# Output projection's first steps in old pools and its last group in another order; a beginning by half channels with eight buffers

## The chip, the cores and the metric

One of the eight cores of a Trainium2 chip runs the whole kernel. The metric is device time in microseconds. A core has five engines that run side by side and meet by semaphores: TensorE (PE) multiplies matrices into PSUM, VectorE (DVE) and ScalarE (ACT) work element by element, GpSimd (POOL) takes smaller work, and SyncE (SP) issues most DMAs. ACT and POOL can issue DMAs too. Each engine executes its own instructions strictly in order.

## The reference

One step of a layer for a prompt of 1024 rows and 8 samples of 8 rows each (1088 rows, 1024 channels, float32):

```
mod = silu(c) @ w_ada + b_ada                     # 6 sections of 1024 columns
h   = rms_norm(x) * (1 + scale1) + shift1
p   = h @ w_in                                    # z, xbc, dt | qkv, gate, beta, alpha
y   = SSD scan of silu(conv(xbc)), gated by silu(z), grouped norm     # 1024 rows of "mixed"
o   = gated delta rule of silu(conv(qkv)), norm, gated by silu(gate)  # the other 1024
x   = x + gate1 * rms_norm(concat(y, o) @ w_out)
x   = x + gate2 * rms_norm(swiglu(modulated norm of x) @ w_down)
```

It returns x and the new convolution and recurrent states of prompt and samples.

## The kernel before

Activations lie with channels on the 128 partitions, rows along the free axis, in three groups of rows TH of 384, 384 and 320 (the last ends with the 64 sample rows). A float32 product is made of three matmuls: activations and weights are each split into a rounded high part and the remaining low part (hh, hl and wh, wl), and high x high, low x high and high x low are added in PSUM. The split of weights is a cast on ACT (L173) and a subtraction on DVE (L174).

**Order.** PE's instructions run in the order in which the program text issues them (manual_schedule). For the other engines a scheduler orders them; earlier program text has higher priority, and an instruction without open dependences can be placed far ahead of its text. Side work is written as generators in `tasks`; every `tick()`, called at fixed places between matmuls, moves each of them on by one `yield`.

**Beginning.** c, the first three x tiles, w_ada's first four column blocks (2 MB each) and the first weights are loaded by SP; the w_ada tiles `w2` have 12 buffers. `ada_block` makes a block's 512 columns of mod, `ada_cols` (L304) turns them into modT. `turned` (L339) transposes x tiles, `modulated` (L357 to L368) makes hh and hl: one ACT pass, one or two DVE passes, and the low part on DVE (even k) or POOL (odd k). The first two column tiles of w_in (`first`: k and q of head 0) are multiplied while h is still being made: PE runs block 0, block 2, transpositions of channels 0 to 3, block 1, matmuls of channels 0 to 3 (`first_k`, L416 to L418), block 3, then channels 4 to 7. For groups two and three `first_group` interleaves, channel by channel, three transpositions, the modulation and six matmuls two channels behind. `few` adds the small parameters and the halo rows of the convolution (36 small transpositions, L391).

**Output projection.** `gemm_rows` goes through three groups of rows. A group has 16 steps; step k takes 128 rows of the mixed result (`mixed_load` from DRAM, L1331), splits them (sh, sl; L1398, L1399) and multiplies them with two halves of w_out's rows (`w_out_half`, casts L173): 18 matmuls a step (L1386 to L1389), fewer in the last group, and four ticks. All groups go k = 8 to 15 first (the delta rule's), then 0 to 7 (the scan's; these need a multiply by the group norm, L1458). Weights of even k use pool wp, of odd k pool wo; pieces of even k use pool mxp, of odd k g_. wo and g_ lie where the scan's tiles were. `gdn_samples`, the delta rule for the samples, runs in the ticks of groups one and two, and its result is read from DRAM by group three.

Of the kernel before, what the change touches and what calls it, by code (L numbers as in the profile page):

```python
# [8 lines left out]
F32 = mybir.dt.float32  # L9
# [7 lines left out]
P = 128  # L17
# [26 lines left out]
def hybrid_step(ctx: ExitStack, tc: tile.TileContext, x_p, x_s, c_p, c_s, st_ssd, st_ssdc, st_gdn, st_gdnc,  # L44
# [34 lines left out]
    warm = cA.tile([1, 1], F32, name="warm")  # L79
    dve.memset(warm, 0.0)  # L80
    act.activation(out=warm, in_=warm, func=AF.Silu)
# [77 lines left out]
    def bank():  # L159
        return bg[0].tile([P, 512], F32, name="ps")  # L160
# [73 lines left out]
    sp.dma_start(out=cc[0:1, :], in_=c_p)  # L234
    sp.dma_start(out=cc[1:9, :], in_=c_s)
    sp.dma_start(out=cc[9:10, :], in_=n_mix_pre)
# [13 lines left out]
    def load_x(i):  # L250
        n = P if i < NC else NS
        if i >= 4:
            xts.append(init.tile([P, 2, 512], F32, name="w2", bufs=12).rearrange("p a n -> p (a n)"))
        xt = xts[i]
        sp.dma_start(out=xt[0:n], in_=x_p[i * P:(i + 1) * P, :] if i < NC else x_s)
# [9 lines left out]
    for i in range(3):  # L265
        load_x(i)
# [12 lines left out]
    w2s = {}  # L279

    def load_ada(cb):
        w2s[cb] = []
        for k in range(0, KD, 2):
            w2 = init.tile([P, 2, 512], F32, name="w2", bufs=12)
            sp.dma_start(out=w2, in_=w_ada[k * P:(k + 2) * P, cb * 512:(cb + 1) * 512]
                         .rearrange("(a p) n -> p a n", p=P))
            w2s[cb].append(w2)
# [28 lines left out]
    def load_params():  # L316
        sp.dma_start(out=r1[0:8, :], in_=n_mix_pre[0].rearrange("(r c) -> r c", c=P))
        sp.dma_start(out=r1[8:16, :], in_=n_ffn_pre[0].rearrange("(r c) -> r c", c=P))
        sp.dma_start(out=r1[16:24, :], in_=ssd_nw[0].rearrange("(r c) -> r c", c=P))
        sp.dma_start(out=r1[24:25, :], in_=gdn_nw)  # L320
        sp.dma_start(out=r1[25:37, :], in_=ssd_cb[0].rearrange("(r c) -> r c", c=P))
        sp.dma_start(out=r1[37:85, :], in_=ssd_cw[0].rearrange("j (r c) -> (j r) c", c=P))
        sp.dma_start(out=r2, in_=gdn_cw[0].rearrange("j (r c) -> (j r) c", c=P))

    def params():
        ps = bank()
        pe.transpose(ps[:, 0:85], r1[0:85, :], ident[0:85, 0:85])
        pe.transpose(ps[:, 128:224], r2, ident[0:96, 0:96])
        dve.tensor_copy(prm1T, ps[:, 0:85])
        dve.tensor_copy(prm2T, ps[:, 128:224])  # L330
        yield
# [40 lines left out]
    def mod(g, k, ps):  # L372
        c0, n = TH[g]
        modulated(ps, k, c0, n, hh[k][:, c0:c0 + n], hl[k][:, c0:c0 + n], init, pool if k % 2 else dve)


    HALOS = ((st_ssdc[0], 0, 8), (st_ssdc[0], 8, 4), (st_gdnc[0], 0, 8), (st_gdnc[0], 8, 8), (st_gdnc[0], 16, 8))
    sts = []

    def load_halos():  # L380
        for src, a, n in HALOS:
            st = init.tile([P, 2, 512], F32, name="w2", bufs=12).rearrange("p a n -> p (a n)")[0:24, 0:n * P]
            sp.dma_start(out=st, in_=src[:, :, a * P:(a + n) * P].rearrange("b t c -> (b t) c"))
            sts.append(st)

    def halos():
        for st, (src, a, n) in zip(sts, HALOS):
# [24 lines left out]
    def first_k(g, k, pss):  # L412
        t0, n = TH[g]
        xh, xl = hh[k][:, t0:t0 + n], hl[k][:, t0:t0 + n]
        for (hi, lo), o in zip(first, pss):
            pe.matmul(o, lhsT=hi[k], rhs=xh, start=(k == 0), stop=False)  # L416
            pe.matmul(o, lhsT=hi[k], rhs=xl, start=False, stop=False)
            pe.matmul(o, lhsT=lo[k], rhs=xh, start=False, stop=(k == KD - 1))  # L418

    def first_group(g):  # L420

        pss = [ps_a.tile([P, 512], F32, name="ps")[:, 0:TH[g][1]] for _ in first]
        for k in range(KD + 2):
            if k < KD:
                mod(g, k, turned(g, k))
            if k >= 2:
                first_k(g, k - 2, pss)
                tick()
        hid_box[g] = clock[0]
        return pss  # L430

    load_ada(0)
    load_ada(2)
    for load in loads:
        load(0)
    load_ada(1)
    rows = ada_block(0)
    load_ada(3)
    for load in loads:
        load(1)  # L440
# [3 lines left out]
    tps = [turned(0, k) for k in range(4)]  # L444
    ada_cols(2, rows2)
    for k in range(4):
        mod(0, k, tps[k])
    rows = ada_block(1)
    for k in range(2):
        first_k(0, k, first_ps)  # L450
    ada_cols(1, rows)
    for k in range(2, 4):
        first_k(0, k, first_ps)
    rows2 = ada_block(3)
    for i in range(3, NT):
        load_x(i)
    load_params()
    load_halos()

    wsr = gk.tile([P, 4, NS], F32, name="sm").rearrange("p a t -> p (a t)").rearrange("p (k m) -> p k m", m=32)  # L460
    for a, b, c in ((0, 16, C_DT), (16, 24, C_ALPHA), (24, 32, C_BETA)):
        sp.dma_start(out=wsr[:, :, a:b], in_=w_in[:, c:c + b - a].rearrange("(k p) m -> p k m", p=P))
    tps = [turned(0, k) for k in range(4, KD)]
    ada_cols(3, rows2)
    for k in range(4, KD):
        mod(0, k, tps[k - 4])
    with tc.high_priority(-80):
        for i in range(3, NT):
            norm_x(i)
    for k in range(4, KD):  # L470
        first_k(0, k, first_ps)
    hid_box[0] = clock[0]
    wst = gk.tile([P, NP], F32, name="gate")[:, 0:KD * 64].rearrange("p (k m) -> p k m", m=64).bitcast(F32R)

    def rate_weights():
        pool.memset(wst.bitcast(F32), 0.0)
        act.copy(wst[:, :, 0:32], wsr)
        dve.tensor_sub(wst[:, :, 32:64], wsr, wst[:, :, 0:32].bitcast(F32))
        yield

    def few():

        yield from wait(6)
        yield from params()
        yield from halos()
        yield from rate_weights()

    few_run = few()
    spawn(few_run)

# [476 lines left out]
    def first_two(wts):  # L967

        raws = [conv_raw() for _ in wts]
        pss = first_ps  # L970
        for g in range(3):
            if g:
                pss = first_group(g)
            t0, n = TH[g]
            for ps, raw in zip(pss, raws):
                raw[2](ps, t0, n, min(n, NP - t0))
        settle(few_run)
# [351 lines left out]
    def mixed_load(k, c0, n):  # L1329
        t = (g_ if queue and k % 2 else mxp).tile([P, 384], F32, name="mx", bufs=3)  # L1330
        sp.dma_start(out=t[:, 0:n], in_=mixdr[k * P:(k + 1) * P, c0:c0 + n])  # L1331
        return t

# [13 lines left out]
    KS = list(range(KD, 2 * KD)) + list(range(KD))  # L1347

    queue, last = [(k, *TH[gi]) for gi in range(2) for k in KS], []
    for i in range(4):  # L1350
        ahead.append(mixed_load(*queue.pop(0)))
# [111 lines left out]
    def gdn_samples():  # L1463
        smx = g_.tile([P, HG, 4, NS], F32, name="smx")
        sp.dma_start(out=smx, in_=smdr)
# [10 lines left out]
        yield from wait(16)  # L1476
# [238 lines left out]

    def w_out_half(k, hf):
        return load_half(w_out[k * P:(k + 1) * P, hf * 512:hf * 512 + 512], wp=wo if k % 2 else wp)

    ph_f = ExitStack()
    for gi, grp in enumerate(GRP):  # L1720
# [22 lines left out]
        gemm_rows(grp, KS, w_out_half, mixed_piece(c0, n), mid, done)  # L1743
        if gi == 1:
            settle()
            last += [(k, *TH[2]) for k in KS]
            for i in range(2):
                ahead.append(mixed_load(*last.pop(0)))
# [224 lines left out]
```

## Time and profile before

| | |
|---|---|
| time, median of 3 runs | 2013.7 us (2012.06 to 2014.39) |
| profiled execution: time, span | 2012.82 us, 2011.0 us |
| PE busy, share of the span | 1951.5 us, 97% |
| DVE, ACT, POOL busy | 67%, 51%, 6% |
| mean granted clock of PE | 0.987 of 2.4 GHz |
| moved by DMA, over the span | 117 GB/s |

Matmuls overlap, so PE busy over a stretch says that it had work, not how fast it went; what a stream of them costs is the distance of their starts. A line of the timeline gives the start, the duration, the engine, the line of the program, the operation, the tiles written and read, and in brackets the idle time before it and what ended it. PEclk is 1.00 at 2.4 GHz and 0.50 at 1.2 GHz.

### The profile page before, as it was taken

What the parts mean: (1) busy time and instruction counts of PE and PEld (TensorE: products, weight loads), DVE (VectorE), ACT (ScalarE), POOL (GpSimd) and SP (SyncE); (2) the same over time, 40 slices, a digit from 0 to 9 for tenths busy, and PEclk for the clock granted to TensorE, in tenths of its full rate; (3) what the DMA queues carried; (4) which work ended last, traced back from release to release, by engine and by line L of the source; (5) the groups of instructions that cost most, each with busy time, mean ns of one, the idle gap of its engine ahead of it and who ended that gap; (6) DMA issues with size and microseconds to landing.
All of it is one profiled execution on the core that took longest, in us unless ns stands there. A gap on an engine that the chain in (4) does not pass through costs nothing.

```text
span 2011.0 us, 35475 instructions
## 1 busy us (share of the span) xinstructions
PE 1951.5 (97%) x13211; PEld 1753.8 (87%) x13211; DVE 1351.1 (67%) x2964; ACT 1035.2 (51%) x2578; POOL 125.9 (6%) x184
## 2 busy tenths in 40 slices
PE   6999999999999999999969999999999999999998
PEld 4898899999999998998857677899999999988886
DVE  4669767877887766867657767885555556645465
ACT  4455455554655446777435666753333334544454
POOL 2100000000000001100011010100000000000000
PEclk9799999999999999999989999999999999999999
DMA  8223323322211127555267855422222224633131
GB/s 300 56 60 102 97 81 110 100 81 87 84 52 55 59 83 189 177 138 159 77 212 228 258 184 192 127 75 81 75 76 82 76 81 128 225 125 110 46 100 50
DMA packets 223142, 235.29 MB, mean 117 GB/s; under 512 B 19018, under 2 KB 177252, under 8 KB 222842
## 3 DMA queue, kind: packets, MB, share of 16 engines
q1 hardware_dynamic: 220266, 228.86, 36.8%
q10 hardware_dynamic: 2384, 3.05, 0.4%
q8 instruction: 104, 1.70, 0.3%
q0 software_dynamic: 320, 1.12, 0.2%
q14 instruction: 68, 0.56, 0.1%
HBM read 188.83 MB, written 44.15 MB: 116 GB/s over the span
## 4 chain that ended last, share of the span: by engine, by line
PE 84%; DVE 6%; ACT 3%; DMA 3%; issue 2%; SPq 1%; POOL 1%; DVEq 0%; POOLq 0%; ACTq 0%
PE ps L198 9%; PE ps L199 8%; PE ps L200 8%; PE ps L1874 7%; PE ps L1873 7%; PE ps L1875 7%; PE ps L1386 7%; PE ps L1389 7%; PE ps L1388 6%; PE ps L741 2%; PE ps L795 1%; DMA wr<-in_w_out_dram 1%; PE ps L704 1%; DVE uc L891 1%; DMA L<-accr 1%
## 5 line engine op out<-in xcount | busy, mean ns | idle before, releaser
L198 PE MATMUL ps<-hh,wh 128*128 128x384 f32 (+1 forms) x1200 | 425.6, 355 | 0.1
L200 PE MATMUL ps<-hh,wl 128*128 128x384 f32 (+1 forms) x1200 | 393.0, 327 | 0.0
L199 PE MATMUL ps<-hl,wh 128*128 128x384 f32 (+1 forms) x1200 | 392.6, 327 | 0.0
L1386 PE MATMUL ps<-wh,sh 128*128 128x512 f32 x678 | 274.6, 405 | 16.0 <-ACT wh L173 15.2
L1389 PE MATMUL ps<-wl,sh 128*128 128x512 f32 x678 | 267.7, 395 | 0.2 <-DVE wl L174 0.2
L198 PEld LDWEIGHTS ps<-hh,wh 128*128 128x128 f32 x1200 | 227.1, 189 | 17.1 <-issue 11.5
L1388 PE MATMUL ps<-wh,sl 128*128 128x512 f32 x604 | 237.6, 393 | 3.7 <-DVE sl L1399 3.7
L199 PEld LDWEIGHTS ps<-hl,wh 128*128 128x128 f32 x1200 | 227.3, 189 | 0.8
L200 PEld LDWEIGHTS ps<-hh,wl 128*128 128x128 f32 x1200 | 226.0, 188 | 0.0
L173 ACT CAST wh<-wr 128x512 fp32r<-128x512 f32 x200 | 122.7, 621 | 171.0 <-PE ps L199 84.5
L174 DVE TENSOR_TENSOR wl<-wr,wh 128x512 fp32r<-128x512 f32 x200 | 136.8, 691 | 58.5 <-ACT wh L173 57.8
L1386 PEld LDWEIGHTS ps<-wh,sh 128*128 128x128 f32 x678 | 128.4, 189 | 52.4 <-ACT wh L173 15.6
L174 DVE TENSOR_TENSOR wl<-wd,wh 128x512 fp32r<-128x512 f32 x130 | 89.6, 692 | 118.1 <-ACT wh L173 114.8
L1389 PEld LDWEIGHTS ps<-wl,sh 128*128 128x128 f32 x678 | 128.4, 189 | 30.3 <-DVE wl L174 0.8
L173 ACT CAST wh<-wd 128x512 fp32r<-128x512 f32 x130 | 80.7, 621 | 139.0 <-PE ps L1388 100.3
L1388 PEld LDWEIGHTS ps<-wh,sl 128*128 128x128 f32 x604 | 114.5, 190 | 27.3 <-DVE sl L1399 4.5
L1810 ACT CAST wh<-s 128x512 fp32r<-128x512 f32 x104 | 64.4, 620 | 83.1 <-PE ps L1874 74.6
L1873 PE MATMUL ps<-T_0h,wh 128*128 128x272 f32 x352 | 102.0, 290 | 3.3 <-DVE u L1889 1.8
L1874 PE MATMUL ps<-T_0l,wh 128*128 128x272 f32 x352 | 101.6, 289 | 0.0
L1874 PE MATMUL ps<-T_1l,wh 128*128 128x272 f32 x352 | 101.6, 289 | 0.0
L1875 PE MATMUL ps<-T_0h,wl 128*128 128x272 f32 x352 | 101.3, 288 | 0.0
L1875 PE MATMUL ps<-T_1h,wl 128*128 128x272 f32 x352 | 101.3, 288 | 0.0
(496 smaller groups left out, 4442.6 us busy)
## 6 DMA issues: line engine op xcount, KB each, us to landing
wr<-in_w_in_dram SPq DMA_DIRECT2D x104, 256.0 KB
wr<-in_w_gate_up_dram SPq DMA_DIRECT2D x104, 256.0 KB
wr<-in_w_out_dram SPq DMA_DIRECT2D x96, 256.0 KB
w<-in_w_ada_dram SPq DMA_DIRECT2D x16, 1024.0 KB
wd<-in_w_down_dram SPq DMA_DIRECT2D x22, 512.0 KB
actdr<-as SPq DMA_DIRECT2D x18, 544.0 KB
L<-accr SPq DMA_DIRECT2D x16, 544.0 KB
am<-actdr SPq DMA_DIRECT2D x44, 192.0 KB
```

What stands on the lines that cost most here:

```text
L173: act.copy(wh, src)
L174: low.tensor_tensor(out=wl, in0=src, in1=wh.bitcast(F32), op=ALU.subtract)
L198: pe.matmul(out, lhsT=hi[k], rhs=xh[k], start=(k == 0), stop=False)
L199: pe.matmul(out, lhsT=hi[k], rhs=xl[k], start=False, stop=False)
L200: pe.matmul(out, lhsT=lo[k], rhs=xh[k], start=False, stop=(k == KD - 1))
L1386: pe.matmul(o, lhsT=sh[:, cs], rhs=wh, start=first, stop=False)
L1388: pe.matmul(o, lhsT=sl[:, cs], rhs=wh, start=False, stop=False)
L1389: pe.matmul(o, lhsT=sh[:, cs], rhs=wl, start=False, stop=last)
L1810: act.copy(wh, opa[p])
L1873: pe.matmul(o, lhsT=wh[:, cs], rhs=bh[:, m, :], start=(m == 0 and not on), stop=False, **on)
L1874: pe.matmul(o, lhsT=wh[:, cs], rhs=bl[:, m, :], start=False, stop=False, **on)
L1875: pe.matmul(o, lhsT=wl[:, cs], rhs=bh[:, m, :], start=False, stop=(m == 3), **on)
```

## The change

The beginning no longer loads the activation table with a tiny SiLU. c, the first x tiles, the parameters, the halo rows and the rate weights are loaded by ACT; w_ada's tiles have 8 buffers and are asked for where they are used. PE takes a group in half channels (`first_half`): transpositions and modulation of four channels, then all their matmuls, tile by tile. Groups two and three are transposed and modulated in `hidden_rest` by ticks and multiplied by the ordinary `third`. In the output projection the first two steps' weights come from wp and their pieces from mxp, three pieces are loaded ahead, the samples' loads come six ticks later (their first use four), and the last group goes k = 0 to 15.

```diff
-    warm = cA.tile([1, 1], F32, name="warm")
-    act.activation(out=warm, in_=warm, func=AF.Silu)
-    sp.dma_start(out=cc[0:1, :], in_=c_p)      # and two more, and x tiles 0 to 2
+    act.dma_start(out=cc[0:1, :], in_=c_p)
     def ada_block(cb, between=None):
         for k in range(0, KD, 2):
-            w2 = w2s[cb][k // 2]
+            w2 = init.tile([P, 2, 512], F32, name="w2", bufs=8)
+            sp.dma_start(out=w2, in_=w_ada[...])
     def params():
+        act.dma_start(out=r1[0:8, :], in_=n_mix_pre[0]...)   # and six more
+        yield from wait(3)
+    def hidden(g, step, ks=range(KD)):
+        for k in ks:
+            ps = turned(g, k)
+            modulated(ps, k, ...)
+            if k % step == step - 1:
+                yield
+        if KD - 1 in ks:
+            hid_box[g] = clock[0]
     def halos():
+            st = gk.tile([P, NP], F32, name="vT", bufs=1)[0:24, 0:n * P]
+            act.dma_start(out=st, in_=src[...])
+            yield from wait(2)
+    def hidden_rest():
+        for i in range(3, NT):
+            norm_x(i)
+        yield from wait(5)
+        yield from hidden(1, 3)
+        yield from hidden(2, 3)
+    def first_half(h):
+        for _ in hidden(0, KD, range(4 * h, 4 * h + 4)):
+            pass
+        for (hi, lo), o in zip(first, first_ps):
+            for k in range(4 * h, 4 * h + 4):
+                # the three matmuls of first_k for this tile and channel
+                if h:
+                    tick()
     rows = ada_block(0)
     ...
     rows2 = ada_block(2, lambda: ada_cols(0, rows))
+    for load in loads:
+        load(0)
     ada_cols(2, rows2)
+    first_half(0)
     rows = ada_block(1)
-    (first_k of channels 0 to 3, ada_cols(1), ada_block(3), channels 4 to 7 as above)
+    rows2 = ada_block(3, lambda: ada_cols(1, rows))
+    for load in loads:
+        load(1)
+    ada_cols(3, rows2)
+    (loads of x tiles 3 to 8 by SP, of the rate weights wsr by ACT)
+    spawn(params())
+    spawn(later(halos(), 4))
+    spawn(hidden_rest())
+    first_half(1)
     def first_two(wts):
-        for g in range(3):
-            if g:
-                pss = first_group(g)
-            ...
+        for ps, raw in zip(first_ps, raws):
+            raw[2](ps, *TH[0], TH[0][1])
+        for g in range(1, 3):
+            for wt, raw in zip(wts, raws):
+                third(wt, g, raw[2])
-    KS = list(range(KD, 2 * KD)) + list(range(KD))
+    KS = [list(range(KD, 2 * KD)) + list(range(KD))] * 2 + [list(range(2 * KD))]
+    queue = [(gi, k) for gi in range(3) for k in KS[gi]]
     def mixed_load(...):
-        t = (g_ if queue and k % 2 else mxp).tile([P, 384], F32, name="mx", bufs=3)
+        t = (g_ if gi < 2 and i > 2 and i % 2 else mxp).tile([P, 384], F32, name="mx", bufs=3)
     def mixed_piece(c0, n):
-            if queue or last:
-                ahead.append(mixed_load(*(queue or last).pop(0)))
+            while asked[0] < len(queue) and len(ahead) < (3 if asked[0] < 4 * KD else 2):
+                mixed_load()
     def gdn_samples():
+        yield from wait(6)
         sp.dma_start(out=smx, in_=smdr)
-        yield from wait(16)
+        yield from wait(14)
     def w_out_half(k, hf):
-        return load_half(..., wp=wo if k % 2 else wp)
+        steps[0] += 1
+        return load_half(..., wp=wo if steps[0] > 4 and steps[0] % 4 in (1, 2) else wp)
```

## Rows read from the trace of the kernel before

**Rows 1.** Who PE waited for, whole span: us in total, times, longest us.
```profile
PE ps L1386 <- ACT wh L173: 15.2, 1, 15.2
...
PE ps L1388 <- DVE sl L1399: 3.7, 1, 3.7
...
PE ps L417 <- DVE hl L368: 3.2, 3, 1.6
```

**Rows 2.** Stretches of 2 us: length, PE busy (instructions), PEclk, DMA share, GB/s.
```profile
36.00:38.00 2.00, 1.01 (x8) 1.00 1.02 408
...
40.00:42.00 2.00, 2.00 (x8) 0.50 0.21 52
...
46.00:48.00 2.00, 1.21 (x8) 1.00 0.76 57
...
68.00:70.00 2.00, 2.00 (x8) 0.50 0.00 0
...
80.00:82.00 2.00, 2.00 (x9) 0.50 0.87 242
```

**Rows 3.** Timeline of the beginning, up to group two's first transpositions.
```profile
9.68 3.79 PE L277 MATMUL ps<-w,caF 128*32 128x512 f32 x12 [4.41 <-DMA w<-in_w_ada_dram]
...
22.44 0.20 DVE L309 SCALAR_TENSOR_TENSOR modT<-ps,wmix 128x36 f32<-128x36 f32 x1 [0.95 <-PE ps L304]
...
26.75 1.25 POOL L368 TENSOR_TENSOR hl<-ht,hh 128x384 fp32r<-128x384 f32 x1 [0.79 <-DVE ht L359]
...
32.54 1.92 PE L277 MATMUL ps<-w,caF 128*32 128x512 f32 x16
...
36.75 0.20 DVE L309 SCALAR_TENSOR_TENSOR modT<-ps,wmix 128x36 f32<-128x36 f32 x1 [0.93 <-PE ps L304]
...
46.69 0.33 PE L339 MATMUL ps<-ident,w 128*128 128x128 f32 x1 [1.13 <-DVE rs L123]
```

**Rows 4.** Timeline of PE in the beginning: what single operations cost.
```profile
20.08 1.53 PE L339 MATMUL ps<-ident,kq 128*128 128x128 f32 x12
...
50.34 0.52 PE L416 MATMUL ps<-hh,wh 128*128 128x384 f32 x1
...
50.66 0.52 PE L417 MATMUL ps<-hl,wh 128*128 128x384 f32 x1
...
78.10 1.04 PE L391 MATMUL ps<-ident,w 24*128 24x24 f32 x8
...
86.47 0.31 PE L417 MATMUL ps<-hl,wh 128*128 128x320 f32 x1
86.61 0.30 PE L418 MATMUL ps<-hh,wl 128*128 128x320 f32 x1
```

**Rows 5.** Timeline of the output projection's first two steps.
```profile
999.88 0.60 ACT L173 CAST wh<-wr 128x512 fp32r<-128x512 f32 x1
...
1003.46 0.51 PE L1386 MATMUL ps<-wh,sh 128*128 128x512 f32 x1
...
1011.92 0.42 SPq L1465 DMA_DIRECT2D smx<-smdr  x1
...
1015.64 1.07 SPq L181 DMA_DIRECT2D wr<-in_w_out_dram  x2
...
1023.07 0.79 PE L1386 MATMUL ps<-wh,sh 128*128 128x512 f32 x1 [15.20 <-ACT wh L173]
```

**Rows 6.** Chain of work that ended last: start, us, what.
```profile
79.14 0.93 PE ps L339 x3
...
1015.64 6.74 DMA wr<-in_w_out_dram
...
1027.61 1.89 PE ps L1265 x18
```

**Rows 7.** A stretch of group three: length, PE, PEld, DVE, ACT, POOL busy, PEclk.
```profile
1237.00:1242.00 5.00, 1.28 (x7) 0.73 (x5) 5.00 (x11) 4.37 (x10) 0.00 (x0) 0.94 0.01 2
```

**Rows 8.** Groups of DVE's instructions by line, 1187 to 1245 us: busy us, mean ns.
```profile
L1458 DVE SCALAR_TENSOR_TENSOR mx<-mx,prm1T,RB 128x320 f32<-128x320 f32 x5 | 2.8, 550 | 3.8 <-DMA mx<-mixdr 3.8
```

More of the change, by code (lines that the diff above doesn't have):

```diff
@@ L277, in ada_rows @@
             pe.matmul(ps[r], lhsT=caF[:, k, :], rhs=w(k), start=k < 4, stop=k >= 4)
[L279 to L287, printed above, removed]
     def ada_block(cb, between=None):
@@ L370, in hybrid_step @@
     hid_box = {}
-    def mod(g, k, ps):
+    def hidden(g, step, ks=range(KD)):
         c0, n = TH[g]
[L374 to L384, printed above, removed]
-    def halos():
-        for st, (src, a, n) in zip(sts, HALOS):
+        for k in ks:
+            ps = turned(g, k)
+            modulated(ps, k, c0, n, hh[k][:, c0:c0 + n], hl[k][:, c0:c0 + n], init,
+                      pool if k % 2 else dve)
+            if k % step == step - 1:
+                yield
+        if KD - 1 in ks:
+            hid_box[g] = clock[0]
+    def halos():
+        for src, a, n in ((st_ssdc[0], 0, 8), (st_ssdc[0], 8, 4), (st_gdnc[0], 0, 8), (st_gdnc[0], 8, 8),
+                          (st_gdnc[0], 16, 8)):
+            st = gk.tile([P, NP], F32, name="vT", bufs=1)[0:24, 0:n * P]
+            act.dma_start(out=st, in_=src[:, :, a * P:(a + n) * P].rearrange("b t c -> (b t) c"))
+            yield from wait(2)
             ps = bank()
@@ L410, in hybrid_step @@
     first_ps = [ps_a.tile([P, 512], F32, name="ps")[:, 0:TH[0][1]] for _ in first]
[L412 to L436, printed above, removed]
+    def first_half(h):
+        for _ in hidden(0, KD, range(4 * h, 4 * h + 4)):
+            pass
+        t0, n = TH[0]
+        for (hi, lo), o in zip(first, first_ps):
+            for k in range(4 * h, 4 * h + 4):
+                xh, xl = hh[k][:, t0:t0 + n], hl[k][:, t0:t0 + n]
+                pe.matmul(o, lhsT=hi[k], rhs=xh, start=(k == 0), stop=False)
+                pe.matmul(o, lhsT=hi[k], rhs=xl, start=False, stop=False)
+                pe.matmul(o, lhsT=lo[k], rhs=xh, start=False, stop=(k == KD - 1))
+                if h:
+                    tick()
     rows = ada_block(0)
-    load_ada(3)
-    for load in loads:
-        load(1)
     for i in range(3):
@@ L467, in hybrid_step @@
[L467 to L472, printed above, removed]
-    wst = gk.tile([P, NP], F32, name="gate")[:, 0:KD * 64].rearrange("p (k m) -> p k m", m=64).bitcast(F32R)
[L475 to L486, printed above, removed]
@@ L1346, in hybrid_step, with mixed_load @@
     late_box = {}
-    KS = list(range(KD, 2 * KD)) + list(range(KD))
-    queue, last = [(k, *TH[gi]) for gi in range(2) for k in KS], []
-    for i in range(4):
-        ahead.append(mixed_load(*queue.pop(0)))
+    KS = [list(range(KD, 2 * KD)) + list(range(KD))] * 2 + [list(range(2 * KD))]
+    queue = [(gi, k) for gi in range(3) for k in KS[gi]]
+    asked = [0]
+    def mixed_load():
+        i = asked[0]
+        asked[0] += 1
+        gi, k = queue[i]
+        c0, n = TH[gi]
+        t = (g_ if gi < 2 and i > 2 and i % 2 else mxp).tile([P, 384], F32, name="mx", bufs=3)
+        sp.dma_start(out=t[:, 0:n], in_=mixdr[k * P:(k + 1) * P, c0:c0 + n])
+        ahead.append(t)
+    for i in range(3):
+        mixed_load()
     def load_gains(i, gp, gs):
@@ L1714, in second_half @@
         yield from flips(GRP[1][1:], t, 2 * HN, 6 * P)
+    steps = [0]
     def w_out_half(k, hf):
-        return load_half(w_out[k * P:(k + 1) * P, hf * 512:hf * 512 + 512], wp=wo if k % 2 else wp)
+        steps[0] += 1
+        return load_half(w_out[k * P:(k + 1) * P, hf * 512:hf * 512 + 512],
+                         wp=wo if steps[0] > 4 and steps[0] % 4 in (1, 2) else wp)
     ph_f = ExitStack()
@@ L1741, in done @@
             return after
-        gemm_rows(grp, KS, w_out_half, mixed_piece(c0, n), mid, done)
+        gemm_rows(grp, KS[gi], w_out_half, mixed_piece(c0, n), mid, done)
         if gi == 1:
             settle()
-            last += [(k, *TH[2]) for k in KS]
-            for i in range(2):
-                ahead.append(mixed_load(*last.pop(0)))
             ph_s.close()
```

65 lines of the change are left out of this document (22 added, 43 removed).

## The prediction

> **What bounds the kernel now.** I read the page's busy shares first: the tensor engine (PE) is busy 97% of a 2011.0 us span, so at most some 60 us of idle time and the stretches at the lower clock can be won or lost. Then I read who PE waited for, over the whole span: two waits in the output projection stand out, 15.2 us for a cast of weights and 3.7 us for a split of activations [rows 1]. Then the beginning in stretches of 2 us. Until about 38 us the DMA engines are full (share 1.02 at 408 GB/s), so the first matmuls are paced by w_ada; from then to 86.9 us PE alternates transpositions and matmuls, and from 68 to 82 it is busy throughout at 0.50 of its clock, the 1.2 GHz level [rows 2]. Last the timelines of the beginning and of the first steps of the output projection, with the chain beside them [rows 3 to 6], and the stretch of the second wait [rows 7, 8]. Everything else in the kernel is untouched.
>
> The profiled execution took 2012.82 us, the median of the three timed runs is 2013.7. I sum against 2012.82 and move the result up by 0.9.
>
> **Output projection, first steps.** Step one (k=8) runs on PE from 1003.46 until 1007.87, 18 matmuls. Then PE idles 15.2 us until the cast of step two's weights [rows 5]. Those weights sit in pool wo, whose memory the scan has just left. SP asks for them only at 1015.64, behind the samples' loads (1011.92), and they take 6.74 us to land [rows 5, 6]. In the new kernel step two has its weights in wp and its activations in mxp. The wp loads run far ahead: the cast at 999.88 is of the second half of what wp holds after k=8, ready before step one begins. So step two follows step one at once, about 1007.9 to 1012.3 (4.4 us, like step one), and the 18 small matmuls of the group norm, 1.89 us at 1027.61 [rows 6], which hang on the same ticks, go with it if their sum of squares is ready, which it is by about 1010.5. Step three (k=10) is now the first in wo, and waits as step two did. The ticks put the samples' three loads (tick 7, in the middle of step two) still ahead of step three's weights, which are asked for after tick 8. SP is also held to 1010.6 by the same waits for freed wp buffers as now. So I leave the first cast from wo at about 1022.5, the stall shrinks to some 8 to 10 us, and what is won is the work now inside it: step two's 4.2 (step one's 4.4 without the last matmul's drain) plus 1.9, **-6.1**. Bounds: nothing, or a loss of 0.6 (one more split on VectorE ahead of the wp casts), if step three's weights come later by as much as is won; at best the whole 15.2 and the time at half clock behind it, up to 5 us, -20.
>
> **Last group in another order.** In it PE idles 3.7 us, and from 1237 to 1242 VectorE is busy all 5.0 us [rows 7]: the sums for the next stage and the normalisation of the k<8 pieces meet there. With the order 0 to 15 the pieces there are k>=8 and need no normalising multiply. Four pieces at 0.55 us [rows 8] are 2.2 us less for VectorE, and the split that PE waits for is in that queue: **-2.2**. Bounds: 0 and -5 (the whole wait and the slow matmuls behind it). The multiplies move to 1187 to 1227, where VectorE has time free. If that cover failed it would cost the same 2.2.
>
> **Samples later, loads three ahead.** The samples' work ends four ticks (one step, under 5 us) later. Group three no longer asks for its result before its ninth step, 30 us on. There are 120 ticks in two groups (15 steps of 4 in each) and the work needs 110, so nothing is left over for the end of group two. I take 0, with 1.5 either way for where its pieces meet the group's edge. Three piece loads ahead instead of four still give over 8 us for a load: 0.
>
> **Beginning, up to modT(3).** The warm-up load of the activation table goes (1.3 us behind the first SiLU). It is covered: the first w_ada matmul waited 4.41 us for its weights [rows 3]; without that cover 1.3. c, x and the small loads are issued by ACT, so w_ada starts up to 2 us earlier, but the engines are full until 38 us and carry the same bytes: 0 to -1. Eight buffers hold two blocks, and each is freed before the one that needs it. The real edit is the order on PE. Now the chain of modulation, from modT at 22.44 to the last split's end at 28.0, lies beside block 1, which is paced by DMA anyway, and 24 matmuls follow. Then it stands bare: tile one's matmuls wait for each piece, tile two's twelve end near 30.3, block 1 (1.92 us) and block 3 with the columns between (1.92 + 1.3) run on data already there, to 35.4 against 34.46 now [rows 3]. So the columns of block 3 come 1 us later at full clock. PE would idle for most of 4 us, and in the one like it now (busy 1.01 of 2 from 36 to 38) the clock stood at 0.50 right after [rows 2]: I add 1.5. Bounds 0 and +5 (all of it at half clock). The rate weights' three loads (rows of 64 and 32 bytes) stand at 46 to 48 us, where the engines are 0.76 busy for 57 GB/s [rows 2]; over 44 to 52 they cost about 2.8 us of all engines. ACT may now issue them early, into the full stretch: 0 to +2.8, and I take 1, since block 3 would wait only for what exceeds its slack. Sum **+3.5** at this point.
>
> The Trainium skill, "DMA: Bandwidth & Descriptors", section "Issuing engines are not separate DMA queues", says that DMAs started by different engines run on the same 16 engines and interleave, and that only issue time is saved. By it the small loads take their whole 2.8 us from w_ada and the sum below would be -4.0. No row here shows two loaded queues against each other.
>
> **Beginning, groups two and three.** Group two's first transposition is set by the norm of tile 5 (46.69, [rows 3]), which can absorb about 2 of the 3.5: I take 48.2. From there the work is the same, in another order: 48 transpositions (0.13 each at full clock, 0.31 at half), 48 matmuls of 384 columns (0.32 apart at half clock) and 48 of 320 (0.14 apart at full), by their columns 0.17 and 0.27 at the other level, and 36 halo transpositions (0.13 at half) [rows 4, 6]. Now it ends at 86.91 [rows 4]. Then all transpositions come before or inside the first tile of group two, so I price them, those 24 matmuls and two halo tiles at half clock: 14.9 + 7.7 + 2.1 = 24.7, to 72.9; then 24 matmuls, half of them still slow, 5.9, and 48 at full clock with three halo tiles 8.0: 86.8. Waits of matmuls for single pieces, 2.6 us, a little under the 3.2 that they are now [rows 1], make it 89.4: **+2.5** against now. Bounds: at full clock the chain of 16 modulations (VectorE about 1.0 and 1.25 us each) ends near 66 and the last matmuls near 75, -12; all at half clock about 101, +14.
>
> **Sum:** -6.1 - 2.2 + 2.5 = -5.8: 2012.82 - 5.8 = 2007.0, against the median 2007.9, say 2008.
>
> **Rivals.**
> A: more is won. Step three's weights get ahead of the samples' loads on SP, so the stall nearly goes (-10 to -13 instead of -6.1), or the dense matmuls without transpositions bring the clock up early at the beginning (-8 instead of +2.5): about -12 to -16, 1999. For it: the loads do move by ticks, and once the transpositions were done, the matmuls at 86.47 were 0.14 apart again [rows 4]. Against it: tick 7 comes before tick 8, and SP issues by program order once memory is free.
> B: the beginning eats the gain. Modulation and norms on ACT and VectorE, now ahead of the matmuls in bursts, cost the beginning 7 to 9: 2013 to 2014, no change.
> C: slower. The beginning stays at half clock from block 1 to the last matmul of group three. Then modT(3) comes 5 later, the first transposition at 51, and 48 x 0.31 + 48 x 0.32 + 48 x 0.27 + 4.7 = 48, plus 2 of waits, end at 101: +14 - 8.3 = +6, 2019.6. It decides at 95.2 us, where the beginning costs the 8.3 won later. For it: 14 us of busy PE at 0.50 today with the same kinds of work. Against: the last 72 matmuls are dense.
> D: the edit doesn't start step two earlier, because its activations or casts come late behind the scan's tail on ACT and VectorE; then only 2.2 is won against 2.5, no change. Against it: the cast at 999.88.
>
> **How the numbers follow.** The forecast has 0.42 (its own range 2003 to 2012), A 0.20, B and D together 0.20, C 0.18. A measurement of this kernel can tell about 0.2%, 4 us, from no change. The forecast falls short of that in about a tenth of all cases: faster 0.53, within 0.28, slower 0.19. Two tenths are left out at the ends of A and C: 1997 to 2019.
>
> **What would show it.** Right: step two's matmuls follow step one's without a gap, and PE's longest wait is 7 to 11 us, before step three; the 3.7 us wait in the last group is under 2.5; the last matmul of the first two tiles ends between 86 and 92. Wrong: that matmul ends after 95 (C) or before 80 (A); a wait under 4 us before step three (A); a gap behind step one (D); a new wait over 3 us at a group's edge or for a piece load.

## The result, and the profile after

The changed kernel takes 1995.3 us (median of 4 runs, 1990.6 to 1999.5) against 2014.05 beside it: ratio 0.9907, 95% interval 0.9883 to 0.9931. That is 18.8 us won where 5.8 were forecast, and below the range by 1.7. Run again twice on other chips it had 0.9911 (0.9895 to 0.9927) and 0.9920 (0.9905 to 0.9934).

The profiled execution took 1990.57 us, span 1988.8. Who PE waited for, over the whole span:

```profile
PE ps L265 <- ACT gate L235: 7.8, 1, 7.8
PE ps L1350 <- ACT wh L170: 7.3, 1, 7.3
PE ps L416 <- DVE hl L355: 3.2, 2, 2.2
...
PE ps L1556 <- DVE s_ut L1547: 2.4, 1, 2.4
PE ps L326 <- DVE ht L346: 2.4, 3, 1.8
```

The 15.2 us of [rows 1] are 7.3, the 3.7 us are gone, and 2.4 at L1556 are new. (The 7.8 stands at the kernel's very start: PE waits for the SiLU of c, whose table load now comes only after c has landed. The first w_ada matmul still starts at 9.21, against 9.68 in [rows 3].) The chain of waits at the output projection's first steps has the same form as before [rows 6]:

```profile
999.79 0.42 SPq L1430
1000.27 0.64 SPq L1438
1000.95 1.07 SPq L1440
1002.06 1.48 SPq L1311
1003.58 6.66 DMA wr<-in_w_out_dram
1010.27 0.63 ACT wh L170
1010.94 0.80 PE ps L1350
```

L1430 to L1440 are the samples' loads, and step three's weights are asked for behind them, as forecast. The chain is no shorter: from the first of these loads to the matmul at its end it is 11.15 us here (999.79 to 1010.94) and was 11.15 before (1011.92 to 1023.07, [rows 5]). What is shorter is PE's wait, because step two now runs beside the chain. The beginning: modT(3), PE's first transposition of group two, the last matmul of the first two tiles, the first of the rates (the matmuls for dt, alpha and beta, which follow the first two tiles):

```profile
40.78 0.20 DVE L298 SCALAR_TENSOR_TENSOR modT<-ps,wmix 128x36 f32<-128x36 f32 x1
```
```profile
49.85 0.27 PE L326 MATMUL ps<-ident,kq 128*128 128x128 f32 x1
...
80.00 0.31 PE L197 MATMUL ps<-hh,wl 128*128 128x320 f32 x1
...
81.70 0.34 PE L470 MATMUL ps<-hh,gate 128*64 128x384 f32 x1
```

modT(3) comes 4.0 later than in [rows 3]. Group two's first transposition comes 4.7 later: in the kernel before it stands at 45.18, and the 46.69 of [rows 3] is the third, the one that waited for the norm of tile 5:

```profile
45.18 0.27 PE L339 MATMUL ps<-ident,kq 128*128 128x128 f32 x1
```

Yet the end at 80.3 is 6.6 earlier than 86.9 [rows 4]. In between the clock differs. Stretches of PE (length, busy, granted clock, and behind it DMA share and GB/s), first of the changed kernel, then the slow one of the kernel before:

```profile
48.00:52.00 4.00, 4.00 (x30) 0.88 1.11 342
52.00:56.00 4.00, 2.24 (x17) 1.00 0.11 39
56.00:60.00 4.00, 3.41 (x20) 1.00 0.06 16
...
68.00:72.00 4.00, 4.00 (x29) 1.00 0.09 25
...
80.00:84.00 4.00, 4.00 (x26) 1.00 0.46 112
```
```profile
66.00:84.00 18.00, 17.75 (x77) 0.53 0.12 30
```

From group two's first transposition to the rates the kernel before takes 43.6 us; 4.9 of them PE is idle, and 10.2 it loses because, busy, it runs at 0.50. The changed kernel takes 31.9, with 2.4 idle and nothing lost to the clock.

To set all kernels side by side I read five milestones in each profile's timeline, to about 0.1 us: when the rates' first matmul starts; from there to step one of the output projection; from there to the end of step three; from there to the 90th matmul of the last group; and that group's next 144 matmuls.

```
                rates   to step 1  3 steps  to group 3  in group 3
before          88.73     914.7     33.4      181.9       43.3
after           81.70     911.0     24.6      183.6       38.1
e1_begin        82.30     913.8     33.8      183.4       44.3
e2_out          88.36     916.1     25.5      183.8       38.3
e3_oldlast      82.17     910.6     25.5      188.3       42.0
e4_noticks      82.68     915.4     25.8      185.0       37.6
e5_inter        93.11     916.7     25.5      184.9       37.6
e6_halos        84.06     915.7     34.3      182.0       41.9
e7_hidden       88.07     913.6     34.6      181.7       41.7
e8_ticks12      84.01     914.1     18.9      197.6       37.6
e9_after        85.31     911.3     25.8      183.8       38.2
e10_norm8       80.86     911.2     34.1      181.5       40.6
e11_rows1       82.77     912.0     20.2      191.4       38.1
e12_gains       83.75     912.1     21.2      188.2       37.6
e13_both        81.45     918.5     25.4      185.1       38.1
e14_both_halos  79.92     912.3     25.7      184.5       37.6
e15_after       83.61     914.6     25.2      184.0       38.7
```

The first, third and fifth columns follow the edits. The second doesn't: nothing is changed there, and it varies by 8 us; single short dips of the clock make up to 5.1 of them (three dips), and PE's idle time varies from 7.3 to 11.0. e13 has three that the profiled execution of the changed kernel hasn't (e13 first):

```profile
95.00:100.00 5.00, 5.00 (x23) 0.66 0.01 3
780.00:785.00 5.00, 3.88 (x16) 0.66 0.52 135
880.00:885.00 5.00, 5.00 (x24) 0.66 0.23 57
```
```profile
95.00:100.00 5.00, 5.00 (x33) 1.00 0.02 6
780.00:785.00 5.00, 5.00 (x56) 1.00 0.30 80
880.00:885.00 5.00, 5.00 (x36) 1.00 0.10 29
```

Of the 22.2 us between the two profiled executions 3.7 lie in this column, where the kernel before lost 3.4 to two dips and the changed kernel nothing. So the medians' 18.8 is the better measure of the change.

### The profile page after: what moved, and what is told of

It reads as the page before. It is cut to its first block, busy times and chain, and to the rows that moved or that the text cites. A ratio compares the mean times of both kernels' runs of the same rounds, so it can differ in the third digit from the quotient of the medians.

```text
span 1988.8 us, 35454 instructions
## 1 busy us (share of the span) xinstructions
PE 1937.0 (97%) x13211; PEld 1743.8 (88%) x13211; DVE 1351.9 (68%) x2963; ACT 1035.1 (52%) x2577; POOL 127.6 (6%) x184
## 4 chain that ended last, share of the span: by engine, by line
PE 84%; DVE 5%; ACT 4%; DMA 4%; issue 1%; SPq 1%; POOL 0%; DVEq 0%; POOLq 0%; ACTq 0%
PE ps L195 9%; PE ps L196 9%; PE ps L197 9%; PE ps L1350 8%; PE ps L1353 7%; PE ps L1840 7%; PE ps L1839 7%; PE ps L1841 7%; PE ps L1352 6%; PE ps L701 2%; PE ps L755 1%; DVE uc L851 1%; PE ps L809 1%; DMA L<-accr 1%; DMA w<-in_w_ada_dram 1%
## 5 line engine op out<-in xcount | busy, mean ns | idle before, releaser
L195 PE MATMUL ps<-hh,wh 128*128 128x384 f32 (+1 forms) x1232 | 435.8, 354 | 0.0
L197 PE MATMUL ps<-hh,wl 128*128 128x384 f32 (+1 forms) x1232 | 402.1, 326 | 0.0
L196 PE MATMUL ps<-hl,wh 128*128 128x384 f32 (+1 forms) x1232 | 402.0, 326 | 0.0
L195 PEld LDWEIGHTS ps<-hh,wh 128*128 128x128 f32 x1232 | 232.3, 189 | 17.0 <-issue 12.3
L196 PEld LDWEIGHTS ps<-hl,wh 128*128 128x128 f32 x1232 | 232.5, 189 | 0.8
L197 PEld LDWEIGHTS ps<-hh,wl 128*128 128x128 f32 x1232 | 231.2, 188 | 0.0
L171 DVE TENSOR_TENSOR wl<-wr,wh 128x512 fp32r<-128x512 f32 x200 | 136.1, 690 | 56.2 <-ACT wh L170 55.7
L1777 DVE TENSOR_TENSOR wl<-wr,wh 128x512 fp32r<-128x512 f32 x78 | 53.8, 691 | 70.4 <-ACT wh L1776 69.2
L1839 PE MATMUL ps<-T_1h,wh 128*128 128x272 f32 x352 | 101.2, 287 | 0.3 <-ACT as L1846 0.3
```

The lines of the kernel that those rows point to most:

```text
L171: low.tensor_tensor(out=wl, in0=src, in1=wh.bitcast(F32), op=ALU.subtract)
L195: pe.matmul(out, lhsT=hi[k], rhs=xh[k], start=(k == 0), stop=False)
L196: pe.matmul(out, lhsT=hi[k], rhs=xl[k], start=False, stop=False)
L197: pe.matmul(out, lhsT=lo[k], rhs=xh[k], start=False, stop=(k == KD - 1))
L1839: pe.matmul(o, lhsT=wh[:, cs], rhs=bh[:, m, :], start=(m == 0 and not on), stop=False, **on)
```

## The experiments

### The two halves: e1, e2

```
e1: the kernel before with the change's edits up to first_two()
e2: the kernel before with the change's edits from mixed_load() on
```

> The kernel before with the new beginning alone (its loads, its eight buffers, its order up to the end of the first two column tiles); the output projection as before. Theory one: the new order on the tensor engine keeps its clock up, so the last matmul of the first two tiles ends near 80 instead of 86.9 us, the dip at 100 to 106 us goes too, and the time falls by 8 to 11 us to 2003 to 2006. Rival (the price of the prediction): the beginning costs 2 to 4, 2016 to 2018, and what is seen in the changed kernel comes from elsewhere. Second rival: the clock of the beginning is a matter of the single execution; then the time lies between 2006 and 2014 and the profile can show either clock.

> The kernel before with the new output projection alone (first two steps' weights in the old pools, activations three ahead, samples' loads six ticks later, last group from k=0 up); the beginning as before. Theory one: the two parts add up, so this one gives the rest, -9 to -12: 2002 to 2005, with one wait of 7 to 8 us before step three and none of 3.7 in the last group. Rival (the prediction's terms, -6.1 and -2.2): 2005.5 to 2007. Second rival: the early clock dips of the beginning also shift the output projection's waits, and the parts don't add: outside 2001 to 2007.

e1: 2006.4 us (10 runs, 2000.9 to 2013.3), ratio 0.9964 (0.9947 to 0.9981). e2: 2003.7 (6 runs), 0.9954 (0.9940 to 0.9968). Both medians lie within what theory one said or 0.4 beside it, and -7.3 and -10.0 make -17.3 of the 18.8: within the noise the parts add. e1's rates start at 82.30, e2's at 88.36. The dip near 100 us did not go with the beginning; e1 has it at 95.

### The last group's order, and the six ticks: e3, e4

```diff
-    KS = [list(range(KD, 2 * KD)) + list(range(KD))] * 2 + [list(range(2 * KD))]
+    KS = [list(range(KD, 2 * KD)) + list(range(KD))] * 3
```

> The changed kernel with its last group of the output projection in the old order, k=8 to 15 and then 0 to 7. Theory one: the order is what removed the wait, and it is worth the 5 us by which the lead grows in that group: 1999 to 2001, a wait of 3 to 4 us for a split back in the second half of that group. Rival: the wait went because the samples' work moved; then no wait and 1994 to 1997. The prediction's term was 2.2: 1997 to 1998.

1998.25 (4 runs, 0.9921, 0.9889 to 0.9952), 42.0 us in the last group against 38.1, and the wait is back:

```profile
PE ps L1352 <- DVE sl L1363: 2.7, 1, 2.7
```

The time lies nearer to the prediction's 2.2 than to the 5 that theory one said, though the interval of the ratio overlaps that of the changed kernel. Within the group the order is worth 3.9, and it is what took the wait away. VectorE is as full as before in such a stretch (5.00 of 5 us, as in [rows 7]), but PE no longer stands behind it (length; PE, PEld, DVE, ACT, POOL busy; clock):

```profile
1215.00:1220.00 5.00, 5.00 (x23) 4.09 (x23) 5.00 (x10) 4.47 (x10) 0.00 (x0) 1.00 0.02 8
```

e4:

```diff
         smx = g_.tile([P, HG, 4, NS], F32, name="smx")
-        yield from wait(6)
...
-        yield from wait(14)
+        yield from wait(16)
```

> The changed kernel without the six ticks by which the samples' loads were put off (their work behind the loads starts two ticks later instead, as in the kernel before). Theory one: the loads are ahead of step three's weights on SyncE either way, and they only move from behind step two's weights to ahead of them; step two's weights stand in pools that are full by then, so the wait before step three stays at 6 to 9 us and the time at 1994 to 1998. Rival: the delay is what makes the first steps gain more than the prediction's 6.1: a gap of 2 us or more behind step one, the wait before step three again beyond 9, and 1998 to 2002.

1996.6 (4 runs, 0.9917, 0.9897 to 0.9937), the wait before step three 7.5: theory one.

```profile
PE ps L1350 <- ACT wh L170: 7.5, 1, 7.5
```

The 2.4 us wait at L1556 is not in this kernel; another of 1.4 for a piece of the samples' work (s_ko) is, and one of 1.3 for POOL that the kernel before has too (1.4). The way to the last group is no shorter than with the ticks (185.0): they won nothing and lost nothing.

### What keeps the clock up: e5, e6, e7, e10

e5, groups two and three of the changed kernel in the old order (first_group(), first_k() and mod() as in the kernel before):

```diff
     def hidden_rest():
         for i in range(3, NT):
             norm_x(i)
-        yield from wait(5)
-        yield from hidden(1, 3)
-        yield from hidden(2, 3)
+        yield
...
-        for g in range(1, 3):
-            for wt, raw in zip(wts, raws):
-                third(wt, g, raw[2])
+        pss = first_ps
+        for g in range(3):
+            if g:
+                pss = first_group(g)
+            t0, n = TH[g]
+            for ps, raw in zip(pss, raws):
+                raw[2](ps, t0, n, min(n, NP - t0))
```

> The changed kernel with groups two and three of the first two tiles on the tensor engine in the old order (for each piece its transpositions, then the six matmuls of the piece two before), everything ahead of them and the output projection as changed. Theory one (the order of these two groups is what keeps the clock at full speed): the engine falls to 0.50 for some 10 to 17 us in them, the rates' first matmul starts at 88 to 92 instead of 81.7, and the time is 2002 to 2006. Rival one (the later loads and the bare chain ahead of them shift when the engine idles, and that is what spares the clock): no such stretch, 81 to 84, 1994 to 1998. Rival two (the halos' small transpositions): they come two ticks apart here as in the changed kernel; a stretch only where they stand.

2009.0 (10 runs), 0.9981 (0.9967 to 0.9995), rates at 93.11, 11.4 later than in the changed kernel. Theory one, by more than it said, but the clock is not all of it: up to the rates 5.0 of the 11.4 are time that PE, busy, loses at 0.50, about 3.8 are more idle time (waits for single pieces), and 3.0 a later start of group two.

```profile
52.00:56.00 4.00, 2.44 (x18) 1.00 0.29 107
56.00:60.00 4.00, 3.33 (x14) 0.71 0.02 4
60.00:64.00 4.00, 4.00 (x28) 0.87 0.07 25
...
72.00:76.00 4.00, 2.63 (x11) 0.84 0.09 25
76.00:80.00 4.00, 4.00 (x16) 0.50 0.00 0
80.00:84.00 4.00, 4.00 (x25) 0.81 0.00 0
```

e6, on the kernel before:

```diff
         yield from params()
-        yield from halos()
         yield from rate_weights()
+        yield from wait(40)
+        yield from halos()
```

> The kernel before with the 36 small transpositions of the halos taken out of group three and put behind it, in one piece. Theory one (transpositions and matmuls piece by piece hold the clock down, with or without the halos): the clock still falls near 67 us and the rates start between 86 and 90; 2010 to 2015. Rival two (the halos, 24 columns each, are what holds it down): it comes back within 4 us of its fall, the rates start at 80 to 84, and the time is 2005 to 2009.

2009.3 (10 runs), 0.9988 (0.9974 to 1.0003); rates at 84.06. From 68 to 76, all at 0.50 before, the clock is 1.00, and it dips only at 80:

```profile
64.00:68.00 4.00, 2.26 (x12) 1.00 0.01 2
68.00:72.00 4.00, 4.00 (x26) 1.00 0.00 0
72.00:76.00 4.00, 2.98 (x17) 1.00 0.49 131
76.00:80.00 4.00, 3.41 (x31) 1.00 0.00 0
80.00:84.00 4.00, 4.00 (x32) 0.71 0.51 89
```

Rival two held for the rates to within 0.1, though the ratio's interval touches 1: without the small transpositions between the matmuls, one stretch of 17.1 us at 0.50 (67 to 84) is one of 3.4 (from 81.7). PE's idle time grew by 1.4, so the rates gained less than the clock gave. These transpositions are not enough by themselves to bring the clock down: in the changed kernel they stand between matmuls as well (in pieces of 4 and 8, from 63.9 to 79.2), at 1.00 throughout.

e7, on the kernel before, leaves everything but the order of groups two and three:

```diff
...
+    def hidden_rest():
+        yield from hidden(1, 3)
+        yield from hidden(2, 3)
+
+    spawn(hidden_rest())
     for k in range(4, KD):
         first_k(0, k, first_ps)
+        tick()
...
+        for g in range(1, 3):
+            for wt, raw in zip(wts, raws):
+                third(wt, g, raw[2])
```

> The kernel before with only groups two and three of the first two tiles in the new order (the transpositions of three pieces at a time, then each tile's 24 matmuls in a row); loads, buffers, group one and the output projection as before. Theory one: the clock stays at 1.00 from 54 us on, the rates start at 78 to 80 (the changed kernel's 81.7 less the 3.2 by which its group two begins later), and the time is 2002 to 2006. Rival one: without the later start the clock falls as before; 86 to 90 and 2010 to 2016.

2010.4 (10 runs), 0.9996 (0.9983 to 1.0009), rates at 88.07: theory one missed, and both numbers are those of rival one. But the clock did not fall as before: from 68 us on it was 1.00. PE stood 5.6 us before group three's transpositions, now ahead of all of tile one's later matmuls, for the norm of tile eight, which the old code gives a low priority, and three times, 5.1 us in all, for norms before group two's:

```profile
PE ps L339 <- DVE w L263: 5.6, 1, 5.6
PE ps L339 <- DVE rs L123: 5.1, 3, 3.2
```

e10 adds this to e7:

```diff
-    with tc.high_priority(-80):
-        for i in range(3, NT):
-            norm_x(i)
+    for i in range(3, NT):
+        norm_x(i)
```

> The kernel before with groups two and three in the new order, as in the run that left the rates at 88.07, but with the norms of tiles three to eight in program order instead of at low priority. In that run PE stood 5.6 us before group three's transpositions for the norm of tile eight, which VectorE did after all of group two's pieces; from the first tile's matmuls on the clock was 1.00. Theory (the wait alone undid the order's gain): no wait over 3 us, the rates start at 80 to 83.5, and the time is 2004 to 2008. Rival (the dense order is worth nothing without the changed kernel's loads and front): the rates start at 86 or later, 2009 to 2014.

2003.5 (4 runs), 0.9949 (0.9932 to 0.9966), rates at 80.86, with 1.00 from 52 us on:

```profile
48.00:52.00 4.00, 4.00 (x23) 0.73 1.07 256
52.00:56.00 4.00, 3.53 (x21) 1.00 0.06 16
56.00:60.00 4.00, 3.87 (x22) 1.00 0.02 4
...
80.00:84.00 4.00, 4.00 (x25) 1.00 0.98 324
```

Theory. The order of these two groups, with the norms where it needs them, gives the beginning's whole gain, and the changed loads and buffers none of it. The norms' place alone was not run; it can hardly carry the 7.9 us, since in the kernel before PE waits for a norm only 1.1 us in these groups. The profiles of this section side by side, from group two's first transposition to the rates (lost: what PE, busy, loses by running at 0.50):

```
          length    idle    lost
before      43.6     4.9    10.2
after       31.9     2.4     0.0
e5          40.2     6.2     5.0
e6          38.6     6.3     2.9
e7          44.3     7.6     5.7
e10         36.8     2.5     2.1
```

Each row is one execution; e10's 2.1 lie before 51 us. In e2, with the old order too, 10.2 are lost as before; in the nine profiles with the changed beginning it is never more than 1.7.

### Chasing the 7.3 us: e8, e11, e12

All on the changed kernel; each line is added to the one above it.

```diff
e8   gdn_samples():  -        yield from wait(6)
                     +        yield from wait(12)
...
                     -        yield from wait(14)
                     +        yield from wait(8)
e11  rows_late():    -        yield from wait(2)
                     +        yield from wait(1)
e12  rows_late():             late_box["RB"] = clock[0]
                     +        yield from wait(24)
```

> The changed kernel with the samples' three loads put off by twelve ticks instead of six, and the work behind them starting at the same tick as now. Theory one (step three's weights land late because 1.4 MB of the samples' loads stand ahead of them on SyncE): with these loads behind step three's weights the 7.3 us wait falls under 4, the stretch at half clock behind it goes or shrinks, and the time falls by 3 to 5 us against the changed kernel, to 1990 to 1993. Rival (the weights are held by the pool's memory or by the writes of the scan's tail, not by the loads ahead): the wait stays at 6 to 8 us, 1994 to 1998.

2004.8 (10 runs), 0.9966 (0.9952 to 0.9980): 9 slower than the changed kernel. The wait before step three fell to 1.6, as theory one said, and the three steps to 18.9 us; but from there into group three it took 197.6 instead of 183.6, with 12.4 us of idle time instead of 3.7. PE's waits, then VectorE's:

```profile
PE ps L1353 <- DVE wl L171: 8.5, 3, 6.2
PE ps L1350 <- ACT wh L170: 1.6, 1, 1.6
```
```profile
DVE mx L1422 <- DMA RB<-rsdr: 7.8, 1, 7.8
```

VectorE's multiply of the first k<8 piece waits for the broadcast of the norm's factors (RB), and the split of PE's weights is queued behind it.

> The changed kernel with the samples' loads at twelve ticks and the transposition of the group norm's factors one tick earlier, that is, ahead of step three's matmuls on PE and not behind its third. With the loads at twelve ticks alone the wait before step three fell from 7.3 to 1.6 us, and another of 6.2 came, for weights that VectorE split only after the multiply that waits for the factors' broadcast (landed 1025.8). Theory (the factors are late because their transposition stands on PE behind step three): the broadcast starts at 1007 to 1010 instead of 1020, the 6.2 us wait goes, and the time is 1986 to 1993. Rival (the DMA engines are full from 1000 to 1022 and every load that comes earlier delays another): a wait of 4 us or more at another step, 1995 to 2003.

> The same with the loads of the gains (0.75 MB, needed only at the end of the first group) 24 ticks later. If the engines being full is what moves the wait from place to place, this takes 0.75 of some 8 MB out of the crowded stretch: waits in the first 9 steps of the output projection under 3 us in sum and 1985 to 1990. If not: as the run without it, within 2 us.

e11: 2002.1 (6 runs), 0.9942 (0.9926 to 0.9957); RB is asked for at 1014.2, not 1007 to 1010, and PE has a wait of 4.1 for a later cast: the rival. e12: 1998.6 (6 runs), 0.9936 (0.9919 to 0.9953), waits of 3.8 in the first nine steps, a little over the 3 said:

```profile
PE ps L1351 <- ACT wh L170: 2.6, 2, 1.4
PE ps L1470 <- DVE s_ko L1451: 1.0, 1, 1.0
```

The time is not the 1985 to 1990 that was said, nor within 2 us of e11, and not below the changed kernel's 1995.3 beside it. The DMA engines are still full in these microseconds (1.03 and 1.13 below), the lead of 3.4 us after three steps is lost again by step six, and what matmuls there are run at half clock:

```profile
1005.00:1010.00 5.00, 3.76 (x12) 0.57 1.03 374
1010.00:1015.00 5.00, 4.84 (x12) 0.50 1.13 312
```

### Repeats and the best of both: e9, e13, e14, e15

e9 and e15 are the changed kernel itself. e13 is e10 with e2's output projection; e14 is e13 with e6's edit.

> The changed kernel as it is, once more, beside the kernels of this call. Every profile so far shows a handful of short dips of the clock to 0.50 at places that differ from execution to execution (near 100, 235, 780, 880 us); the profiled execution of the changed kernel had none of them, and led by 22.2 us where the medians differ by 18.8. Theory (those dips are chance, the beginning and the output projection are not): a median of 1994 to 1998, the rates' first matmul again at 81 to 83 us, the wait before step three again 7 to 8 us, and one or two such dips. Rival (the early stretch at full speed was chance too): rates at 86 or later in this profile, median 1999 or more.

> The kernel before with the new order of groups two and three (norms in program order) and the new output projection, but the old front of the beginning: loads of c, x and the parameters by SyncE, twelve buffers, transpositions of group one ahead of the columns. Theory (the changed kernel's front costs 1 to 3.5 us, the order alone gives the gain): the rates start at 80 to 82, the output projection's part is as in the changed kernel, and the time is 1991 to 1995, 0.5 to 4 under the changed kernel beside it. Rival (the front costs nothing once the order is new, since VectorE's and ScalarE's chain of modulations sets the pace of group two): within 1 us of it, either way.

> The same with the 36 small transpositions of the halos behind group three. Theory (order and halos are one cause, the clock; with the clock at 1.00 the halos cost 36 x 0.07 = 2.5 us wherever they stand): rates within 1 us of the run without this edit, time the same within 2. Rival (they cost 4.7 by themselves, as in the old order): rates at 75 to 77, and the time 3 to 5 lower.

> The changed kernel beside these two, for comparison on the same chip: 1994 to 1997; rates at 81 to 86.

e9: 1995.3 (4 runs), rates at 85.31, later than the 81 to 83 that was said, with one dip at 80 to 84: the early stretch at full speed is no chance, single dips in it are. e15: 1996.55 (5 runs), rates at 83.61. e13: 1997.15 (6 runs), 0.9922 (0.9907 to 0.9938). Its rates start at 81.45, as the theory said, but its time is within 1 us of e15: the rival; in time the old front is no better than the new one. The gains of e10 and e2 would make -19.3, and e13 has -15.7; its profile has three dips in the second column. e14: 1992.0 (4 runs, 1988.95 to 1992.4), 0.9896 (0.9881 to 0.9910), the lowest of all kernels. Its rates start 1.5 earlier than e13's, between what the two theories said, and that doesn't explain 5 us; the profiles show only fewer dips later (912.3 against 918.5 in the second column). Whether the halos' place has to do with those stays open, and its interval still meets e15's.

## Why the prediction was wrong

**The step that failed** is in groups two and three of the beginning: "Then all transpositions come before or inside the first tile of group two, so I price them, those 24 matmuls and two halo tiles at half clock: 14.9 + 7.7 + 2.1 = 24.7, to 72.9". They ran at full clock, though group two started at 49.85 and not at the 48.2 that I took. From the first transposition at 49.85 to the end of tile one's 24 matmuls at 66.5 it took 16.7, not 24.7; the rest took 13.8, forecast 16.5 with its waits. I had carried 1.2 GHz over from the old order to the new because the kinds of work are the same. The runs show that in these groups the level hangs on how they are mixed: the old order in the changed kernel makes +11.4 at the rates (e5), 5.0 of it by the clock; the new order in the old kernel -7.9 (e10), where the time lost at 0.50 falls by 8.1; the halos out of the old order -4.7 (e6), where it falls by 7.3. Why this mix of work brings the clock down stays open. Over the nine profiles with the changed beginning the rates start at 83.1 on average, 5.4 before the two with the old one (88.5): **-5.4 instead of +2.5**. Rival A named this ("the dense matmuls without transpositions bring the clock up early"), with -8 and a chance of 0.20; C, which would have kept the clock down, was given nearly as much on evidence from the old order alone. By the prediction's own signs the end at 80.3 is neither right (86 to 92) nor A (before 80).

**Up to modT(3)** the sum of +3.5 came out, +4.0 measured, but partly by luck. The bare chain of modulation and the half clock behind it cost all of it: the 24 matmuls end at 34.1, where I had 30.3 at full clock and 1.5 for the clock. The 1.0 for the small loads isn't seen, since PE waited for no weights in blocks one and three. For the next step I took too little: group two's first transposition came 4.7 later, not 1.5, because the tile 5 that I let absorb 2 us held the third transposition and not the first. The Trainium skill's rule on issuing engines ("DMA: Bandwidth & Descriptors", "Issuing engines are not separate DMA queues"), by which loads share the same 16 DMA engines whoever issues them, could not be tested on the small loads, which no run isolates. It agrees with one row: c's rows for the samples, issued by ACT beside SP's loads of w_ada, let ACT go on at 5.37, and at 3.12 when they stood ahead of these on SP. By e13 against e15 the whole front is worth nothing at the end.

**First steps of the output projection**: the mechanism was right in each part. Step two follows step one at once, step three waits 7.3 (7 to 11 said), and its weights stand behind the samples' loads. The size was -6.1; the three steps take 25.4 on average instead of 34.0, **-8.6**. Idle time makes nearly all of it, 15.6 against 7.2 on average. The 6.1 was there; the cast came 1.4 us earlier, seen from step one, than I put it (1010.27 plus the lead of 10.8 is 1021.1, not 1022.5), because SP came to the samples' loads 7.1 us after step one's start and not 8.5. The slow stretch behind the wait gave little: PE, busy, lost 3.5 at 0.50 on average before and 3.1 after. The rest, under 1 us, isn't told apart.

**Last group**: -2.2 forecast, **-4.3** on average (38.0 against 42.3). I priced the four multiplies; what went was nearly the whole wait that goes with the old order (2.7 of idle time on average) and the slow matmuls after it (1.5), near the lower end of my bounds.

**Samples later**: 0 forecast; from step three's end into the last group it takes about **+2**, just over the 1.5 allowed, and it is idle time of PE (2.2 on average before, 4.2 after). The ticks are not the cause: e4, without them, hasn't the wait of 2.4 at L1556 and takes 185.0 all the same, with 4.6 idle. What else in the new output projection costs these 2 us stays open.

Sum of the measured terms: -5.4 - 8.6 - 4.3 + 2.1 = -16.2, against -16.3 to -18.8 between the medians of three sets of runs. (Each average is over the kernels of the table that have that step as before, or as changed; where a further edit or, in e3, a dip reaches into the column, the kernel is left out: e8, e11 and e12 for the first steps, these, e3 and e4 for the samples.)

## What to carry to other kernels

Where a sum hangs on the clock's level, the level is a case with a chance of its own, and the old order's level says nothing sure on a new one: here it changed with what stands between the matmuls. A wait that ends on a transfer in a stretch where the engines are full moves on when that transfer is put ahead (7.3 became 6.2, then 4.1, at other places; that full engines are the reason is argued, not shown); name what comes due next before counting it as won. And compare milestones over several profiles: chance dips of the clock made 3.4 of 22.2 us here.

## What was not expected of the hardware

The clock fell while PE was busy nearly throughout (17.75 of 18 us from 66 to 84 in the kernel before, at 0.53), and stayed at 1.00 through a stretch with 2.24 of 4 us busy in the changed one: the busy share of these stretches doesn't tell which. Short dips come in fully busy stretches too (5.00 of 5 us at 95 and at 880 in e13), each worth 1.7 us. Over all profiles those between the rates and the output projection stand at four places (95 to 105, 227 to 242, 781 to 783, 872 to 884 us), and executions of one kernel differ in which of them they have: the changed kernel's first profile has none, its third two. The kernel before spread from 2005.6 to 2020.0 us over 31 runs on one chip; how much of that is dips isn't shown.
